# Group norm of the RWKV layer: sums, squares and normalisation moved from wide VectorE operations to ScalarE in blocks of 64 columns

## The chip, the cores and the metric

The kernel runs on one core of one Trainium2 chip. The metric is the device time of one execution in microseconds (us). PE is the matrix engine (TensorE), DVE VectorE, ACT ScalarE, POOL GpSimd, SP the engine that here only issues transfers.

## The reference

A decoder trunk of two residual layers, one sequence of 512 tokens, width 2048, all float32. Layer 0 is gated differential attention, layer 1 a gated RWKV-7 time mixing with 32 heads of 64. Layer 1, cut to what matters:

```python
p = h @ w_in;  p = p + (token_shift(p) - p) * mu       # r, k, v, g, and low-rank parts
y = wkv7_scan(r, decay, k, v, -kk, kk * a)             # (512, 32 heads, 64)
mean = jnp.mean(y, axis=-1, keepdims=True)
var = jnp.mean(jnp.square(y - mean), axis=-1, keepdims=True)
y = (y - mean) * lax.rsqrt(var + GN_EPS)
y = y * gn_w + gn_b + jnp.sum(r * k * r_k, axis=-1, keepdims=True) * v
out = (y * silu(g)) @ w_out
```

The change concerns the mean, the variance and the normalisation of `y`, per token and head.

## The kernel before

**Layer 1.** `layer1` runs over 16 pairs of heads (j = 0 to 15); the two heads of a pair have 128 channels. For each pair `unit_chan` makes four projections (k, r, v, gate) of 128 columns each, in matmuls of 128x512. Each product of float32 is three matmuls of split operands: `split_w` takes a loaded weight block `wraw`, writes its rounded part `wh` on ACT (L105) and the rest `wl` on DVE (L106), two buffers of each. `shift_mix` takes a projection out of PSUM and mixes it with its shifted self (L1187 on ACT, L1188 on DVE: mixr, mixk, mixv). `stage1` and `stage2` make the decays `E` and the tiles `AR` and `BK`; AR's second half (L1334) needs mixr.

**Gram and solve.** `gram` multiplies BK with AR in 16 matmuls (L1361), ACT copies the four results into `G` (L1368), and two blocks of G and the key norms `ssl` go through DRAM (`ltd`) into the tile `LT`, issued by POOL (L1407). `t_solve` inverts triangular blocks of 32 by a chain of small DVE operations that starts at L1409 and ends at L1429 (L1420 and L1422 by turns). The result goes through DRAM again (`td`, L1430, and `TT`, L1449, both issued by SP).

**The scan of the pair before.** A `Chain` is a generator whose steps are put in among the projections' matmuls, after a given number of them. `t_combine` transposes TT on DVE (L1459, tile `T1`, two instructions), multiplies with G (L1465, bank `px`), copies the result `X` on ACT (L1468), multiplies again (L1476) and copies it into TT (L1479). `scan_pair` then has eight steps of three matmuls each: L1558 (ACT copies `rhs`, L1561), L1569 with rhs and TT (ACT copies `VS`, L1571), and L1576 (DVE writes the next state VS, L1580 or L1583). After the eighth step `outputs` writes Y, two PSUM banks of 128 tokens x 4 blocks x 64 (L1598, L1602), and `centre` follows.

**The group norm.** `centre` sums Y over 64 columns (L1613, `s1`), scales the sum (L1614) and subtracts it (L1615), all on DVE, into `yc`, 128 tokens x 8 groups x 64. `group_norm` squares yc on ACT in one instruction (L1624), and on DVE sums the squares (L1626), makes `var` (L1627), its reciprocal root `rsg` in 11 small operations (`rsqrt`, L64 to L71), and multiplies (L1630). `finish_y` later transposes yc on PE (L1637) and adds it to the pair's `y`.

**Order.** Each engine's queue is in order. The order is set by a scheduler from the program's text, priorities (`high_priority`, `issue_after`) and its own estimates of durations, so that a change in one place can move instructions of others. `group_norm` of pair j - 2 is called at the head of pair j from j = 4 on.

Of the kernel before, what the change touches and what calls it, by code (L numbers as in the profile page):

```python
# [13 lines left out]
F32 = mybir.dt.float32  # L14
# [3 lines left out]
AF = mybir.ActivationFunctionType  # L18
ALU = mybir.AluOpType
AX = mybir.AxisListType  # L20
# [3 lines left out]
P = 128  # L24
# [3 lines left out]
NT = T // P  # L28
# [29 lines left out]
def rsqrt(g, out, v, n, tag):  # L58

    nc = g.nc  # L60
    m = 1 if tag in ("r4", "r16") else 3 if tag == "r8" else 2
    sh = g.small.tile([P, n], I32, name="rs_i", tag=tag + "i", bufs=m)
    t = g.small.tile([P, n], F32, name="rs_t", tag=tag + "t", bufs=m)
    nc.vector.tensor_single_scalar(sh[:], v.bitcast(I32), 1, ALU.logical_shift_right)  # L64
    nc.vector.tensor_scalar(sh[:], sh[:], -1.0, float(0x5F3759DF), ALU.mult, ALU.add)
    y = sh[:].bitcast(F32)
    for i in range(3):
        nc.vector.tensor_mul(t[:], y, y)
        nc.vector.scalar_tensor_tensor(t[:], t[:], -0.5, v, ALU.mult, ALU.mult)
        o = out if i == 2 else y  # L70
        nc.vector.scalar_tensor_tensor(o, t[:], 1.5, y, ALU.add, ALU.mult)  # L71
# [1120 lines left out]
C = 64  # L1192
NC_ = T // C
HALF = 32
NG = 4
# [351 lines left out]
def scan_pair(g, j, p, gap, gap_s, others):  # L1547
# [8 lines left out]
    for c in range(NC_):  # L1556
# [29 lines left out]
        yield gap_s  # L1586
    outputs(g, j, p)
    centre(g, p)


# [15 lines left out]
def centre(g, p):  # L1606

    nc, w, Y = g.nc, g.work, p.Y
    s1 = g.small.tile([P, NT, 2], F32, name="s1", tag="s1", bufs=3)
    p.yc = w.tile([P, 2 * NT, C], F32, name="yc", tag="yc", bufs=1)  # L1610
    for h in range(2):
        yg = Y[h][:, : NT * C].rearrange("p (t n) -> p t n", t=NT)
        nc.vector.reduce_sum(s1[:, :, h], yg, AX.X)  # L1613
        nc.vector.tensor_scalar(s1[:, :, h], s1[:, :, h], 1.0 / C, None, ALU.mult)  # L1614
        c = nc.vector.tensor_sub(p.yc[:, h::2, :], yg, s1[:, :, h : h + 1].to_broadcast([P, NT, C]))  # L1615
    g.centred = c.ins


def group_norm(g, j, p):
    p.chain.finish(g)  # L1620
    nc, w, yc = g.nc, g.work, p.yc
    NG = 2 * NT
    sq = w.tile([P, NG, C], F32, name="ysq", tag="ysq", bufs=1)
    nc.scalar.activation(sq[:], yc[:], AF.Square)  # L1624
    var = g.small.tile([P, NG], F32, name="var", tag="var", bufs=3)
    nc.vector.reduce_sum(var[:], sq[:], AX.X)  # L1626
    nc.vector.tensor_scalar(var[:], var[:], 1.0 / C, GN_EPS, ALU.mult, ALU.add)  # L1627
    rs = g.small.tile([P, NG], F32, name="rsg", tag="rsg", bufs=3)
    rsqrt(g, rs[:], var[:], NG, "r8")
    nc.vector.tensor_mul(yc[:], yc[:], rs[:, :, None].to_broadcast([P, NG, C]))  # L1630


def finish_y(g, j, p, bank=("pd", 1)):
# [8 lines left out]
def layer1(g, aps):  # L1642
    nc, tc = g.nc, g.tc
    with ExitStack() as cx:
# [32 lines left out]
        for j in range(D // P):  # L1677
# [16 lines left out]
            if normed:  # L1694
                group_norm(g, j - 2, pairs[j - 2])

            def behind(m, j=j, p=p, normed=normed):
                if j > 1:
                    pairs[j - 2].chain.finish(g)
                with tc.issue_after(m.ins):  # L1700
                    gram(g, j, p, j > LAG + 1 and pairs[j - 1].chain)
                with tc.issue_after(g.lower) if normed else ExitStack():
                    p.rfs = split_act(g, p.rf[:], w, "x")
                mask_gram(g, p, 0)
                loaded = t_solve(g, j, p, LAG < j < D // P - 1)
                with tc.issue_after(loaded):
                    mask_gram(g, p, 1)
                if j > 1 and not normed:
                    group_norm(g, j - 2, pairs[j - 2])
# [17 lines left out]
        chain(g, j, p, 24, 4, 5, lead=34)  # L1727
        gps = proj(3, j - 1)
        group_norm(g, j - 1, pairs[j - 1])
        gts = [gate(g, j - 1, gps)]  # L1730

# [140 lines left out]
```

## Time and profile before

| | |
|---|---|
| median of 3 runs (lowest, highest) | 2056.24 us (2054.85, 2058.01) |
| profiled execution, its time and span | 2055.6 us, 2053.9 us |
| granted TensorE clock | 1.0 |
| busy: PE, DVE, ACT, POOL | 99%, 78%, 55%, 19% of the span |
| second layer's pairs | about 1040 to 1930 us of the span |

The span is the time from the first to the last instruction; the profiled execution's own time has the launch around it. Times in the profile's rows count from the span's start. A row of a group of instructions gives the line in the kernel, the engine, the operation, output and inputs with their shapes, the count, then busy time, the mean of one in ns, and the idle time of the engine just ahead of them with what ended it. Rows in order of time give start, duration and, in brackets, the idle time before.

### The profile page before, as it was taken

The numbers are of one execution on the slowest core, as the hardware profiler recorded it, in microseconds if no ns is written. First come the engines' busy times: TensorE is split into PE (matmuls) and PEld (weight loads), VectorE is DVE, ScalarE is ACT, GpSimd is POOL, SyncE is SP. The second block draws the span as 40 slices with busy tenths as digits, with TensorE's granted clock in tenths as the row PEclk, the third lists the DMA queues.
The fourth block names the chain that finished last, engine by engine and source line by source line (L and its number), as shares of the span: only waits on it lengthen the run. The fifth ranks groups of instructions, "written<-read, shape, count | busy, mean of one in ns | idle before, by whom it ended". The sixth has DMA issues, their size and how long they took to land.

```text
span 2053.9 us, 34174 instructions
## 1 busy us (share of the span) xinstructions
PE 2035.2 (99%) x11922; PEld 1673.1 (81%) x11922; DVE 1605.9 (78%) x4100; ACT 1133.6 (55%) x2258; POOL 400.3 (19%) x782
## 2 busy tenths in 40 slices
PE   9999999999999999999999999999999999999999
PEld 7888888888888888888877778888888888877887
DVE  7988988888898977476787888787777888777745
ACT  5765656666666544355565555555555555545423
POOL 1020111102011000121222222322222222231011
PEclk9999999999999999999999999999999999999999
DMA  8487978879787965823333323223333232346676
GB/s 288 156 163 192 182 172 186 164 192 167 190 180 171 274 218 172 175 87 108 103 83 92 94 77 98 92 89 98 98 98 98 87 96 83 111 127 201 212 182 145
DMA packets 159534, 297.76 MB, mean 145 GB/s; under 512 B 64529, under 2 KB 81937, under 8 KB 159361
## 3 DMA queue, kind: packets, MB, share of 16 engines
q1 hardware_dynamic: 110768, 184.39, 28.8%
q0 software_dynamic: 25952, 90.88, 23.2%
q10 hardware_dynamic: 22640, 20.30, 3.1%
q8 instruction: 94, 1.54, 0.3%
q14 instruction: 80, 0.65, 0.1%
HBM read 271.33 MB, written 24.18 MB: 144 GB/s over the span
## 4 chain that ended last, share of the span: by engine, by line
PE 90%; DVE 6%; ACT 2%; issue 1%; DMA 1%; SPq 0%; ACTq 0%; DVEq 0%
PE pp L124 45%; PE pp L574 24%; PE pt L124 5%; PE gp L1361 2%; DVE wl L106 2%; PE sm L1558 1%; PE sc L124 1%; PE o L124 1%; PE sm L1576 1%; PE sm L1569 1%; ACT wh L105 1%; PE Y L1598 1%; PE pt L296 1%; PE z L124 1%; PE pt L1393 1%
## 5 line engine op out<-in xcount | busy, mean ns | idle before, releaser
L106 DVE TENSOR_TENSOR wl<-wraw,wh 128x1024 fp32r<-128x1024 f32 (+1 forms) x286 | 349.7, 1223 | 167.7 <-ACT wh L105 157.0
L105 ACT CAST wh<-wraw 128x1024 fp32r<-128x1024 f32 (+1 forms) x286 | 299.5, 1047 | 237.6 <-PE pp L124 115.8
L124 PE MATMUL pp<-hL,wh 128*128 128x512 f32 x1024 | 413.6, 404 | 0.0
L124 PE MATMUL pp<-hH,wl 128*128 128x512 f32 x1024 | 413.0, 403 | 0.0
L124 PE MATMUL pp<-hH,wh 128*128 128x512 f32 x1024 | 412.3, 403 | 0.2 <-ACT wh L105 0.2
L124 PEld LDWEIGHTS pp<-hH,wh 128*128 128x128 f32 x1024 | 193.1, 189 | 34.5 <-ACT wh L105 0.4
L124 PEld LDWEIGHTS pp<-hL,wh 128*128 128x128 f32 x1024 | 193.1, 189 | 33.5
L124 PEld LDWEIGHTS pp<-hH,wl 128*128 128x128 f32 x1024 | 193.2, 189 | 32.4
L574 PE MATMUL pp<-wh,hH 128*128 128x512 f32 x448 | 176.8, 395 | 0.0
L574 PE MATMUL pp<-wh,hL 128*128 128x512 f32 x448 | 175.8, 392 | 0.0
L124 PE MATMUL pp<-wh,hH 128*128 128x512 f32 x376 | 147.0, 392 | 0.6 <-ACT hH L1147 0.6
L124 PE MATMUL pp<-wl,hH 128*128 128x512 f32 x376 | 147.5, 392 | 0.0
L124 PE MATMUL pp<-wh,hL 128*128 128x512 f32 x376 | 147.3, 392 | 0.1
L1420 DVE SCALAR_TENSOR_TENSOR tmpl<-LT,Tm 128x60 f32<-128x60 f32 (+24 forms) x496 | 134.8, 272 | 13.2
L574 PE MATMUL pp<-wl,hH 128*128 128x512 f32 x448 | 140.3, 392 | 0.0
L1564 POOL COPY SA<-VS 64x64 f32<-64x64 f32 x224 | 55.4, 248 | 397.8 <-DVE VS L1580 375.4
L1422 DVE TENSOR_TENSOR Tm<-Tm,tmpl 128x60 f32<-128x60 f32 (+24 forms) x496 | 103.4, 209 | 11.7
L1561 ACT COPY rhs<-sm 64x64 f32<-64x64 f32 x256 | 53.0, 207 | 84.8 <-PE sm L1558 81.8
L574 PEld LDWEIGHTS pp<-wl,hH 128*128 128x128 f32 x448 | 84.5, 189 | 17.2
L574 PEld LDWEIGHTS pp<-wh,hH 128*128 128x128 f32 x448 | 84.2, 188 | 17.5 <-issue 0.4
L574 PEld LDWEIGHTS pp<-wh,hL 128*128 128x128 f32 x448 | 84.3, 188 | 16.1
L1571 ACT COPY VS<-sm 64x64 f32<-64x64 f32 x256 | 52.9, 207 | 76.2 <-PE sm L1569 70.3
(435 smaller groups left out, 4374.4 us busy)
## 6 DMA issues: line engine op xcount, KB each, us to landing
wraw<-in_rw_w_in_dram SPq DMA_DIRECT2D x128, 512.0 KB
wraw<-in_da_w_in_dram SPq DMA_DIRECT2D x75, 512.0 KB
wraw<-in_da_w_in_dram POOLq DMA_DIRECT2D x28, 512.0 KB, 6.6
wraw<-in_da_w_out_dram SPq DMA_DIRECT2D x26, 512.0 KB
wraw<-in_rw_w_out_dram SPq DMA_DIRECT2D x24, 512.0 KB
Ta<-in_da_w_in_dram POOLq DMA_DIRECT2D x21, 512.0 KB, 5.6
Tb<-in_da_w_in_dram POOLq DMA_DIRECT2D x21, 512.0 KB, 5.7
Tc<-in_da_w_in_dram POOLq DMA_DIRECT2D x21, 512.0 KB, 5.5
```

The source lines that it names most:

```text
L105: a = nc.scalar.copy(hi[:, ks], raw[:, ks])
L106: d = nc.vector.tensor_sub(lo[:, ks], raw[:, ks], hi[:, ks].bitcast(F32))
L124: m = nc.tensor.matmul(out, a, b, start=s, stop=e, skip_group_check=skip)
L296: nc.tensor.transpose(pt[:, c * P : (c + 1) * P], t1s[t][:, c * P : (c + 1) * P], g.ident[:])
L574: m = nc.tensor.matmul(out[t][:], x, wt[lo][:, k, :], start=first, stop=end and lo == 1 and k == KG - 1, skip_group_check=True)
L1361: m = nc.tensor.matmul(gp[h][:, i * P : (i + 1) * P], BK[r_, c0 + i, :, :], p.AR[r_, c0 + i, :, :], start=True, stop=True)
L1393: nc.tensor.transpose(ps[:, i * P : (i + 1) * P], p.BK[:, c0 + i].rearrange("p s t -> p (s t)"), g.ident[:])
L1420: nc.vector.scalar_tensor_tensor(tt, LT[:, i : i + 1, i + 1 :].to_broadcast([P, s, n]), n2[:, i : i + 1], Tm[:, 0:s, i : i + 1].to_broadca ...
L1422: nc.vector.tensor_add(Tm[:, 0:s, i + 1 :], Tm[:, 0:s, i + 1 :], tt)
L1561: nc.scalar.copy(rhs[r_, :], sm[r_, h * C : h * C + C])
L1564: nc.gpsimd.tensor_copy(p.SA[r_, c - 1, :], VS[r_, c, h, :])
L1571: g.copied = nc.scalar.copy(VS[r_, c, h, :], sm[r_, P : P + C])
```

## The change

The sums of Y are accumulated by eight ACT copies of 64 columns (L1612 in the changed kernel), out of PSUM into `yc`, which is no longer centred; one DVE operation turns the eight sums into minus the means (L1614, `p.mean`). Eight ACT squares (L1624) take minus the mean as bias and accumulate the variance. One small DVE product makes minus mean times `rsg` (L1628), and eight ACT instructions (L1630) normalise yc with it as bias and rsg as scale.

```diff
@@ -1606,14 +1606,12 @@
 def centre(g, p):
 
     nc, w, Y = g.nc, g.work, p.Y
-    s1 = g.small.tile([P, NT, 2], F32, name="s1", tag="s1", bufs=3)
+    p.mean = g.small.tile([P, 2 * NT], F32, name="s1", tag="s1", bufs=3)
     p.yc = w.tile([P, 2 * NT, C], F32, name="yc", tag="yc", bufs=1)
-    for h in range(2):
-        yg = Y[h][:, : NT * C].rearrange("p (t n) -> p t n", t=NT)
-        nc.vector.reduce_sum(s1[:, :, h], yg, AX.X)
-        nc.vector.tensor_scalar(s1[:, :, h], s1[:, :, h], 1.0 / C, None, ALU.mult)
-        c = nc.vector.tensor_sub(p.yc[:, h::2, :], yg, s1[:, :, h : h + 1].to_broadcast([P, NT, C]))
-    g.centred = c.ins
+    for i in range(2 * NT):
+        nc.scalar.activation(p.yc[:, i], Y[i % 2][:, i // 2 * C : i // 2 * C + C], AF.Copy,
+                             accum_out=p.mean[:, i : i + 1])
+    g.centred = nc.vector.tensor_scalar(p.mean[:], p.mean[:], -1.0 / C, None, ALU.mult).ins
 
 
 def group_norm(g, j, p):
@@ -1621,13 +1619,15 @@
     nc, w, yc = g.nc, g.work, p.yc
     NG = 2 * NT
     sq = w.tile([P, NG, C], F32, name="ysq", tag="ysq", bufs=1)
-    nc.scalar.activation(sq[:], yc[:], AF.Square)
     var = g.small.tile([P, NG], F32, name="var", tag="var", bufs=3)
-    nc.vector.reduce_sum(var[:], sq[:], AX.X)
+    for i in range(NG):
+        nc.scalar.activation(sq[:, i], yc[:, i], AF.Square, bias=p.mean[:, i : i + 1], accum_out=var[:, i : i + 1])
     nc.vector.tensor_scalar(var[:], var[:], 1.0 / C, GN_EPS, ALU.mult, ALU.add)
     rs = g.small.tile([P, NG], F32, name="rsg", tag="rsg", bufs=3)
     rsqrt(g, rs[:], var[:], NG, "r8")
-    nc.vector.tensor_mul(yc[:], yc[:], rs[:, :, None].to_broadcast([P, NG, C]))
+    nc.vector.tensor_mul(p.mean[:], p.mean[:], rs[:])
+    for i in range(NG):
+        nc.scalar.activation(yc[:, i], yc[:, i], AF.Identity, bias=p.mean[:, i : i + 1], scale=rs[:, i : i + 1])
 
 
 def finish_y(g, j, p, bank=("pd", 1)):
```

ACT, the end of one pair's scan and the head of the next, a period of the middle of layer 1, before. L1468 to L1479 belong to t_combine, L1561 and L1571 to the first step of the scan, L1368 to gram:

```order
L1571 COPY VS<-sm 64x64 x2
L1624 ACTIVATE ysq<-yc 128x512
L105 CAST wh<-wraw 128x1024
L1187 ACTIVATE mixr<-pp,omu 128x512
L1468 COPY X<-px 32x256 x2
L1348 COPY ssl<-pt 128x128
L1156 CAST sHx<-mixr 128x512
L1368 COPY G_14182<-gp 128x8x64 x4
L1479 COPY TT_9496<-px 32x8x32 x2
L105 CAST wh<-wraw 128x1024
L1561 COPY rhs<-sm 64x64 x2
L1571 COPY VS<-sm 64x64 x2
```

and after, where the eight copies and four of the squares come ahead of mixr and the weight cast, and six of the eight normalisations ahead of TT, all eight ahead of rhs:

```order
L1571 COPY VS<-sm 64x64 x2
L1612 ACTIVATE yc,s_14157<-Y 128x64 x8
L1624 ACTIVATE ysq,var<-yc,s_14157 128x64 x4
L1187 ACTIVATE mixr<-pp,omu 128x512
L105 CAST wh<-wraw 128x1024
L1624 ACTIVATE ysq,var<-yc,s_14157 128x64 x4
L1468 COPY X<-px 32x256 x2
L1348 COPY ssl<-pt 128x128
L1156 CAST sHx<-mixr 128x512
L1368 COPY G_14284<-gp 128x8x64 x2
L1630 ACTIVATE yc<-yc,s_14157,rsg 128x64 x6
L1479 COPY TT_9496<-px 32x8x32 x2
```

ACT goes on, after, with the other two normalisations, the next weight cast and the scan's first step:

```order
L1630 ACTIVATE yc<-yc,s_14157,rsg 128x64 x2
L105 CAST wh<-wraw 128x1024
L1561 COPY rhs<-sm 64x64 x2
L1368 COPY G_14284<-gp 128x8x64 x2
L1571 COPY VS<-sm 64x64 x2
```

Two of gram's four copies of G have moved behind rhs. DVE, between the v projection's mix (mixv) and the start of the solve (L1409), before:

```order
L1188 SCALAR_TENSOR_TENSOR mixv<-pp,mu,mixv 128x511
L1491 TENSOR_TENSOR y<-pt,mixv 128x512
L1580 SCALAR_TENSOR_TENSOR VS<-sm,gam,Sg 64x64 x2
L1409 TENSOR_SCALAR LT<-LT 128x32
L1410 RECIPROCAL LT<-LT 128x32
L1420 SCALAR_TENSOR_TENSOR tmpl<-LT,Tm 128x31
```

and after, where a weight split and the state of scan step 2 come ahead of the solve:

```order
L1188 SCALAR_TENSOR_TENSOR mixv<-pp,mu,mixv 128x511
L1491 TENSOR_TENSOR y<-pt,mixv 128x512
L1580 SCALAR_TENSOR_TENSOR VS<-sm,gam,Sg 64x64 x2
L106 TENSOR_TENSOR wl<-wraw,wh 128x1024
L1580 SCALAR_TENSOR_TENSOR VS<-sm,gam,Sg 64x64 x2
L1409 TENSOR_SCALAR LT<-LT 128x32
L1410 RECIPROCAL LT<-LT 128x32
L1420 SCALAR_TENSOR_TENSOR tmpl<-LT,Tm 128x31
```

DVE at the head of a period, after. L1524 and L1531 belong to the gate of an earlier pair, L1459 are the two transposes:

```order
L1429 TENSOR_TENSOR Tm<-Tm,LT 128x256
L1524 SCALAR_TENSOR_TENSOR mixv<-thg,mixv 128x512
L1531 TENSOR_TENSOR mixv<-mixv,y 128x512
L1614 TENSOR_SCALAR s_14157<-s_14157 128x8
L1188 SCALAR_TENSOR_TENSOR mixr<-pp,mu,mixr 128x511
L1459 STREAM_TRANSPOSE T_14189<-TT_9496 64x256
L106 TENSOR_TENSOR wl<-wraw,wh 128x1024
L1459 STREAM_TRANSPOSE T_14189<-TT_9496 64x256
L1334 TENSOR_TENSOR AR<-mixr,E 128x8x64
L1625 TENSOR_SCALAR var<-var 128x8
L1335 SCALAR_TENSOR_TENSOR mixr<-mixr,prm_hrk,f 128x512
```

Before, the two transposes stood together directly behind centre's L1615; now the scaled sums (L1614) stand behind the solve's last instruction, and a weight split stands between the transposes.

## The prediction

> **What bounds the kernel now.** I read the busy shares first, then the busy time by stretch, then the chain that ended last inside one period of the second layer, and then ACT's and DVE's instructions of that period in order of time.
>
> ```profile
> PE 2035.2 (99%) x11922; PEld 1673.1 (81%) x11922; DVE 1605.9 (78%) x4100; ACT 1133.6 (55%) x2258; POOL 400.3 (19%) x782
> ```
>
> ```profile
> 1040.00:1278.00 238.00, 233.02 (x1732) 189.23 (x1732) 190.87 (x534) 132.69 (x311) 64.06 (x158) 1.00 0.32 92
> 1278.00:1808.00 530.00, 530.00 (x3834) 438.89 (x3833) 418.75 (x1160) 294.14 (x674) 142.89 (x342) 1.00 0.33 97
> 1808.00:1930.00 122.00, 119.16 (x807) 93.26 (x806) 86.47 (x216) 60.01 (x136) 27.43 (x59) 1.00 0.54 172
> ```
>
> The second fence is busy time by stretch (length, then PE, PEld, DVE, ACT, POOL, the granted clock, DMA). The change lies in these three stretches. In the middle one, nine equal periods, TensorE is busy for all 530.00 us: nothing done there by another engine can shorten it. TensorE's idle time in the other two is 238.00 - 233.02 = 5.0 and 122.00 - 119.16 = 2.8 us. So the change can gain at most about 8 us, and what it can lose is TensorE time in which the in-order PE queue stands in front of a matmul of the scan whose operand is late. One period of that queue, from the chain that ended last:
>
> ```profile
> 1342.37 0.62 PE px L1465 x32
> ...
> 1343.35 1.99 PE gp L1361 x32
> ...
> 1345.96 2.06 PE pp L124 x8
> ...
> 1349.64 0.17 PE sm L1569 x2
> ```
>
> PE does L1465 (needs DVE's transposes T1), the Gram products, L1476 (needs ACT's X), eight projection matmuls, and at 1349.64 L1569, the first step of the next scan, which needs ACT's TT and rhs. ACT at the same time (start, us, instruction, idle before it):
>
> ```profile
> 1331.80 0.44 ACT L1571 COPY VS<-sm 64x64 f32<-64x64 f32 x2
> 1336.74 0.63 ACT L1624 ACTIVATE ysq<-yc 128x512 f32<-128x512 f32 x1 [4.50 <-DVE yc L1615]
> 1338.10 1.05 ACT L105 CAST wh<-wraw 128x1024 fp32r<-128x1024 f32 x1 [0.73 <-PE pp L124]
> 1339.18 0.69 ACT L1187 ACTIVATE mixr<-pp,omu 128x512 f32<-128x512 f32 x1
> 1343.07 0.74 ACT L1468 COPY X<-px 32x256 f32<-32x256 f32 x2 [3.19 <-PE px L1465]
> ...
> 1344.00 0.62 ACT L1156 CAST sHx<-mixr 128x512 fp32r<-128x512 f32 x1
> 1344.52 2.06 ACT L1368 COPY G<-gp 128x512 f32<-128x512 f32 x4
> 1346.43 0.73 ACT L1479 COPY TT<-px 32x256 f32<-32x256 f32 x2
> 1347.42 1.05 ACT L105 CAST wh<-wraw 128x1024 fp32r<-128x1024 f32 x1 [0.26 <-ACT TT L1479]
> 1348.49 0.43 ACT L1561 COPY rhs<-sm 64x64 f32<-64x64 f32 x2
> 1349.84 0.43 ACT L1571 COPY VS<-sm 64x64 f32<-64x64 f32 x2 [0.93 <-PE sm L1569]
> ```
>
> The reader is to see two things. Up to 1343.07 ACT has 4.50 + 0.73 + 3.19 = 8.4 us of idle time. From 1343.07 to rhs, ending at 1348.92, it has almost none, and PE takes rhs at 1349.64: 0.7 us of slack.
>
> **The prices.**
>
> ```profile
> L1561 ACT COPY rhs<-sm 64x64 f32<-64x64 f32 x256 | 53.0, 207 | 84.8 <-PE sm L1558 81.8
> L281 ACT ACTIVATE t<-t,rr 128x128 f32<-128x128 f32 x64 | 21.2, 393 | 9.0 <-DVE rr L277 9.0
> L1319 ACT ACTIVATE k<-mixk,prm_kk 128x512 f32<-128x512 f32 x16 | 11.5, 721 | 0.3
> L1304 ACT ACTIVATE f<-th,prm_omka,prm_hka 128x512 f32<-128x512 f32 x16 | 12.8, 800 | 0.0
> ```
>
> ```profile
> 344.07 1.28 ACT L281 ACTIVATE t<-t,rr 128x128 f32<-128x128 f32 x4 [0.30 <-DVE rr L277]
> ...
> 377.29 0.46 ACT L350 ACTIVATE a<-sc,nb,sq 128x128 f32<-128x128 f32 x1 [0.87 <-DVE nb L347]
> 377.64 0.19 ACT L350 ACTIVATION_READ_ACCUMULATOR a<-sc,nb,sq 128x1 f32 x1
> 377.74 1.04 ACT L105 CAST wh<-Td 128x1024 fp32r<-128x1024 f32 x1
> ```
>
> No instruction of 64 columns with pointer operands is in this trace, so the prices are estimates from these rows. L1561 is a copy of 64 columns out of PSUM: 0.207 us, which I take for the first eight, since they read PSUM too. With one [128,1] operand L281 (128 columns) and L1319 (512) differ by (721 - 393) / 384 = 0.854 ns a column, so 64 columns take 393 - 55 = 338 ns; that is a square. A second operand adds 800 - 721 = 79: 417 ns, a normalisation. Four L281 in a row take 1.28 us, so each starts (1.28 - 0.393) / 3 = 0.296 after the one before, an overlap of 0.097; a normalisation then occupies 0.32. Where a sum is accumulated, the read follows and the next instruction starts at 377.74, 0.45 after a 0.46 instruction: the read costs the overlap and no more, so copy and square occupy 0.21 and 0.34. Per pair: 8 x 0.21 + 8 x 0.34 + 8 x 0.32 = 7.0 us, in place of one square of 0.63. Over 16 pairs ACT gets about 102 us more.
>
> The Trainium skill, ScalarE: Activation LUTs, section What ACT_TABLE_LOAD costs, gives 186 ns + 0.833 ns a column, 93 ns more for each pointer operand, and 93 ns of overlap back to back. By it the estimate is 8 x (239 + 333 + 333) ns = 7.2 us, with the copies dearer than the 207 ns that the trace has for L1561; the 0.3 us of difference falls on the copies, which lie in idle time, so the sum would stay.
>
> ```profile
> L1613 DVE TENSOR_REDUCE s<-Y x32: 411/416/425, 1047.9 to 1909.0; 128x4 f32<-128x256 f32 x32
> L1615 DVE TENSOR_TENSOR yc<-Y,s x32: 411/416/425, 1049.3 to 1909.9; 128x256 f32<-128x256 f32 x32
> L1630 DVE TENSOR_TENSOR yc<-yc,rsg x16: 681/692/1610, 1055.0 to 1915.3; 128x512 f32<-128x512 f32 x16
> ```
>
> DVE loses 2 x 0.416 + 2 x 0.416 + 0.69, and about as much as the last for the sum of the squares over as many columns: 3.0 us a pair, 49 us in all. It is worth nothing by itself: in the middle stretch DVE is busy 418.75 of 530 us and PE all of it.
>
> **Place 1, from the scan's end to X: hidden.** ACT is free at 1332.24, the outputs Y are complete at 1335.09 (below). Copies to 1336.8, the scaling of the sums on DVE (behind the solve's tail, below), four squares, mixr, the weight cast wh, four squares: 1.7 + 0.3 + 1.4 + 0.6 + 1.05 + 1.4 ends at about 1342, before X can start. The work fits into the 8.4 us of idle time; wh is later, but PE's queue has 32 projection matmuls there, up to 1342.37, that run on the other buffer.
>
> **Place 2, from X to rhs: on the path.** With T the time at which PE can start L1465, DVE's order after it is AR, var, mixr, the rsqrt's small operations with sLx between, and the product of mean and rsg:
>
> ```profile
> 1335.09 0.76 DVE L1613 TENSOR_REDUCE s<-Y 128x4 f32<-128x256 f32 x2 [1.95 <-PE Y L1602]
> ...
> 1338.28 0.17 DVE L1627 TENSOR_SCALAR var<-var 128x8 f32<-128x8 f32 x1
> 1338.48 0.17 DVE L64 TENSOR_SCALAR rs_i<-var 128x8 int32<-128x8 int32 x1
> ...
> 1341.32 0.69 DVE L1334 TENSOR_TENSOR AR<-mixr,E 128x512 f32<-128x512 f32 x1
> ...
> 1342.05 0.75 DVE L1335 SCALAR_TENSOR_TENSOR mixr<-mixr,prm_hrk,f 128x512 f32<-128x512 f32 x1
> ```
>
> Small operations start 0.20 apart, so 13 of them take 2.6, and the three wide ones (two of 0.69, one of 0.75, each overlapping the next by some 0.08) 1.9: mean is ready at T + 4.5. ACT does X, ssl, sHx and two G copies up to T + 0.7 + 1.45 + 1.03 = T + 3.2, and then stands, because its next six instructions are normalisations. They run to T + 4.5 + 1.9 = T + 6.4; TT to T + 7.1; two more to T + 7.8; wh to T + 8.8; rhs to T + 9.2. PE reaches L1569 at T + 1349.64 - 1342.37 = T + 7.3. So PE stands for 1.9 us in each such period, and everything behind it in its queue with it. Bounds: with normalisations as short as L1561 the eight take 0.9 less, 1.0 us; without overlap (0.42 each) and with mean 0.5 late, 3.2 us. I take 1.9, the rows being near. The last two G copies now stand behind rhs, but VS of the next step waits for L1569 anyway, and they feed the Gram exchange, next.
>
> **Place 3, the solve.** In the new DVE order a weight split wl and the scan's VS of step 2 come ahead of the solve's first instruction, L1409:
>
> ```profile
> 1300.29 0.18 DVE L1409 TENSOR_SCALAR LT<-LT 128x32 f32<-128x32 f32 x1
> ...
> 1303.96 1.23 DVE L106 TENSOR_TENSOR wl<-wraw,wh 128x1024 fp32r<-128x1024 f32 x1
> ...
> 1330.04 0.42 DVE L1429 TENSOR_TENSOR Tm<-Tm,LT 128x256 f32<-128x256 f32 x1
> ```
>
> That wl cannot start before 1303.96, since its cast waits for PE to free a buffer; with wl and VS (two of 0.29) the solve starts at 1305.7 instead of 1300.29, 5.4 late. Its body is dense on DVE, one VS step (0.6) fewer and a small split (0.4) more stands in it, and one wl leaves and one enters: it ends 5.2 late. What is late next is the block TT, which goes through two transfers:
>
> ```profile
> 1388.98 0.42 DVE L1429 TENSOR_TENSOR Tm<-Tm,LT 128x256 f32<-128x256 f32 x1
> 1396.18 0.44 DVE L1459 STREAM_TRANSPOSE T<-TT 64x256 f32<-64x256 f32 x1 [0.20 <-DMA TT<-td]
> ```
>
> The period is 1388.98 - 1330.04 = 58.94. The second transpose ends at 1396.6, and PE wants it at 1342.37 + 58.94 = 1401.3: a slack of 4.7. After the change it comes 5.2 late and 1.15 more, because wl now stands between the two transposes: T is 5.2 + 1.15 - 4.7 = 1.7 us late, and PE stands that long before L1465. Bounds: nothing, if the transfers (7.2 us from L1429 to this transpose) run 2 us faster with fewer weight loads ahead of them; 3, if they run as much slower as the trace's other periods differ. I take 1.7. The Gram exchange that feeds the solve is late by its last G copy, at T + 10.2, and must be through before the solve's new, later start; the solve's own 5.4 us and PE's standing cover it.
>
> **Sum.** Eleven pairs (3 to 13) have the new ACT order, ten of them follow a delayed solve: 11 x 1.9 + 10 x 1.7 = 38 us. For the first three and the last two pairs, whose order mixes the same instructions in otherwise, I take two such stalls, 4 us (0 to 8). Together 42 us on the profiled execution's 2055.6, which is 0.6 below the median: 2056.2 + 42 = 2098 us.
>
> **Rivals.**
> - Place 3 costs nothing, because the transfers shrink: 11 x 1.9 + 4 = 25, 2081 us. For it: SP has no load between the two transfers now. Against it: the slack of 4.7 is smaller than the shift of the solve alone. 15%.
> - All of it is hidden: within 4 us, 2056. It needs the normalisations not to stand ahead of TT and rhs; the order says they do, and the slack there is 0.7 us. 6%.
> - Faster. DVE's 3.0 us a pair come off a chain that PE waits on: outside the middle stretch PE's idle 5.0 + 2.8 us vanish, 2048 us. This decides where mean and TT come earlier, not later, that is if the copies took less than DVE's part by over 1 us. 5%. The Trainium skill, Perfetto Trace Analysis, section Optimization Strategies, says to unload the engines that block an idle TensorE; no row of the middle stretch shows such idle time.
> - ACT becomes the bound: all 102 - 10 us that it gets appear in the span, 2148. For it: ACT is in order and feeds PE's weights. Against it: 294 busy of 530 us in the middle stretch, and the 8.4 us of idle time in place 1. 7%.
>
> **How the numbers follow.** My forecast has the other 67%. Its own range, by the bounds above, is 11 x 1.0 + 0 = 11 to 11 x 3.2 + 10 x 3 + 8 = 73 us; ends that all fall together are unlikely, and I take 2068 to 2122, which also takes in the first rival and leaves out 18%. A measurement of this kernel tells apart about 0.2%, 4 us; slower by more than that has 67 + 15 + 7 = 89%, the same 6%, faster 5%.
>
> **What would show it.** Right: a new idle time of PE ahead of L1569, released by ACT's rhs, near 2 us in eleven periods, and one ahead of L1465, released by DVE's transposes; L1409 about 5 us later in its period; ACT without idle time between the scan's end and X; a middle stretch in which PE is no longer busy throughout. Wrong: a span under 2062, PE waiting for the weight casts instead, or normalisations that take far from 0.4 us each.

## The result and the profile after

The changed kernel takes 2129.57 us (median of 4 runs, 2125.92 to 2132.16) against 2055.61 us before (2054.85 to 2058.01): a ratio of 1.0359, 95% interval 1.0346 to 1.0371. It is 74 us slower, where 42 were forecast. The profiled execution took 2132.16 us with a span of 2130.5, 76.6 us longer than the span of before, and that difference is what is taken apart here.

The page's busy line, and the same three stretches of time that the prediction showed of before:

```profile
PE 2069.8 (97%) x11922; PEld 1694.0 (80%) x11922; DVE 1567.3 (74%) x4004; ACT 1236.1 (58%) x2882; POOL 407.2 (19%) x782
```

```profile
1040.00:1278.00 238.00, 229.21 (x1641) 184.67 (x1640) 172.11 (x482) 154.87 (x459) 62.44 (x150) 0.99 0.30 88
1278.00:1808.00 530.00, 500.42 (x3509) 409.32 (x3508) 361.35 (x1010) 318.60 (x941) 133.39 (x309) 0.97 0.29 87
1808.00:1930.00 122.00, 113.15 (x797) 90.04 (x796) 77.55 (x221) 69.95 (x223) 34.65 (x76) 0.96 0.37 110
```

ACT has 102.5 us more and DVE 38.6 less. In the middle stretch PE was busy for all 530.00 us; now it is busy for 500.42, and the column behind POOL, the granted clock, has gone from 1.00 to 0.97. The view by core says the same of the whole span:

```profile
core 0: 2130.5 us, clock 0.987
```

So there are two losses, and a view for each. A stand is here an idle time of PE ahead of one instruction. The waits of PE (who waits, for which line, us in total, times, longest):

```profile
PE sm L1569 <- ACT rhs L1561: 32.0, 13, 3.3
PE px L1465 <- DVE T L1459: 8.5, 7, 2.1
PE sm L1558 <- DVE VS L1580: 7.1, 17, 0.9
```

In the kernel before these three lines had 2.0, 2.0 and 2.8 us. PE's idle time in the span, span less busy, was 2053.9 - 2035.2 = 18.7 us and is 2130.5 - 2069.8 = 60.7: 42.0 us more. The clock is seen in PE's instructions in order of time (start, us, instruction, idle before it), here around one stand ahead of L1569:

```profile
1365.37 0.39 PE L124 MATMUL pp<-hH,wh 128*128 128x512 f32 x1
1365.60 0.39 PE L124 MATMUL pp<-hL,wh 128*128 128x512 f32 x1
1369.13 0.46 PE L1569 MATMUL sm<-rhs,TT 128*128 128x64 f32 x2 [3.15 <-ACT rhs L1561]
...
1369.93 0.63 PE L124 MATMUL pp<-hH,wh 128*128 128x512 f32 x1
1370.35 0.63 PE L124 MATMUL pp<-hL,wh 128*128 128x512 f32 x1
```

Ahead of the stand, matmuls of 512 columns start 0.23 us apart; behind it 0.42. I read the granted clock in stretches of 1 us over the whole span: it is 1.00 or 0.50, and at 0.50 always for 3.41 us or a multiple of that. Sixteen such windows are in this trace, ten single ones between 1178 and 1827, each behind a stand at L1569, one at 1752 behind a wait of 1.33 us at L1465, and five after 1888. A window that PE works through at half rate costs 1.71 us: 27.3 us in all, or 26.6 without the 1.5 us in which PE was idle inside them. The kernel before has none but the last 0.9 us of its span, where PE has no work left. The number is not the same in every execution: of the four runs, the two with a mean clock of 0.987 took 2132 us and the two with 0.990 took 2126 and 2127, and 0.003 of the span, 6 us, would be some four windows (an estimate from these clocks).

42.0 + 27.3 = 69.3 of the 76.6 us. The other 7.3 must be PE time that the profile books as busy. Part of it can be seen: a matmul in front of a stand shows its whole modelled 0.39 us (1365.60) where in a dense queue the next one starts 0.23 after it, so such a stand is about 0.16 us longer than its idle time says. The list has 37 of them at these three lines, 28 more than before: 4.5 us. What is left, some 3 us, is not taken apart.

### The profile page after: what moved, and what is told of

Read it like the earlier page. It is cut to its first block, busy times and chain, and to the rows that moved or that the text cites. A ratio compares the mean times of both kernels' runs of the same rounds, so it can differ in the third digit from the quotient of the medians.

```text
span 2130.5 us, 34746 instructions
## 1 busy us (share of the span) xinstructions
PE 2069.8 (97%) x11922; PEld 1694.0 (80%) x11922; DVE 1567.3 (74%) x4004; ACT 1236.1 (58%) x2882; POOL 407.2 (19%) x782
## 4 chain that ended last, share of the span: by engine, by line
PE 23%; DVE 18%; ACT 5%; DMA 3%; issue 3%; POOL 0%; DVEq 0%; SPq 0%; ACTq 0%; POOLq 0%
PE pp L124 15%; PE pt L124 4%; DVE tmpl L1420 4%; DVE wl L106 3%; DVE Tm L1422 3%; DMA td<-Tm 2%; ACT yc L1630 2%; DVE VS L1580 2%; ACT wh L105 1%; DMA TT<-td 1%; PE sm L1569 1%; PE sm L1558 1%; PE sm L1576 1%; DVE l L1295 1%; PE pt L1393 1%
## 5 line engine op out<-in xcount | busy, mean ns | idle before, releaser
L124 PE MATMUL pp<-hL,wh 128*128 128x512 f32 x1024 | 418.2, 408 | 0.0
L124 PE MATMUL pp<-hH,wh 128*128 128x512 f32 x1024 | 417.5, 408 | 0.1
L124 PE MATMUL pp<-hH,wl 128*128 128x512 f32 x1024 | 417.6, 408 | 0.0
L1420 DVE SCALAR_TENSOR_TENSOR tmpl<-LT,Tm 128x60 f32<-128x60 f32 (+24 forms) x496 | 135.0, 272 | 13.4
L1561 ACT COPY rhs<-sm 64x64 f32<-64x64 f32 x256 | 52.8, 206 | 93.6 <-PE sm L1558 91.2
L1571 ACT COPY VS<-sm 64x64 f32<-64x64 f32 x256 | 52.8, 206 | 69.5 <-PE sm L1569 63.1
```

What stands on the lines that cost most here:

```text
L124: m = nc.tensor.matmul(out, a, b, start=s, stop=e, skip_group_check=skip)
L1420: nc.vector.scalar_tensor_tensor(tt, LT[:, i : i + 1, i + 1 :].to_broadcast([P, s, n]), n2[:, i : i + 1], Tm[:, 0:s, i : i + 1].to_broadca ...
L1561: nc.scalar.copy(rhs[r_, :], sm[r_, h * C : h * C + C])
L1571: g.copied = nc.scalar.copy(VS[r_, c, h, :], sm[r_, P : P + C])
```

## The experiments

Theory A, formed from the two traces: what costs are the queue places, that is the normalisations ahead of TT and rhs on ACT and the later solve on DVE, and the half clock that follows a long stand; the added work itself is free. Theory B: ACT's added 102 us show in proportion, since ACT feeds PE's weights. The first four kernels tell these apart. Theory G, from the fifth on, is A with a rule for the clock: time is divided into windows of 3.41 us on a fixed grid, and a window in which PE was busy for less than half is followed by one at half clock.

**All the work on ACT, the normalisations late.** The changed kernel, but the eight normalisations are issued behind the VS copy of scan step 1, out of the way of rhs, and `finish_y`, which reads them, moves from step 0 to step 3 (not shown).

```diff
+    def normalise():
+        for i in range(NG):
+            nc.scalar.activation(yc[:, i], yc[:, i], AF.Identity, bias=p.mean[:, i : i + 1], scale=rs[:, i : i + 1])
...
+    with tc.issue_after(g.last_copy.ins):
+        q.normalise()
```

> The changed kernel, with the eight normalisations of a pair queued on ACT behind scan step 1 instead of ahead of TT and rhs, and finish_y moved from step 0 to step 3. All of ACT's added work (about 100 us) is still there. Theory A (the time is lost where the normalisations stand ahead of rhs, in the solve that starts later, and in the halved TensorE clock after PE has stood for 3 us): all three vanish, 2055 to 2066 us. Theory B (ACT's added busy time shows in the span in proportion, wherever it stands): still about 2130 us.

Measured: 2069.21 us, ratio 1.0061 (1.0044 to 1.0078). With every instruction of the change on ACT, 61 of 74 us are gone, so B is wrong. The time is above A's range by 3 us. From one L1476 to the next the middle periods last 59.6 to 59.7 us where before they lasted 58.9, some 6 us over the middle stretch, of which 3.3 are idle time. About 5 us more lie in the last pairs, where PE's longest wait is now

```profile
PE pt L1643 <- ACT yc L1632: 3.9, 2, 3.5
```

the late normalisation of a pair whose output PE transposes at 1880, with one window at half clock behind it.

**The sums alone, the squares alone, the normalisation alone.** Each is the kernel before with one third of the change.

```diff
 # sums only (centre)
-    nc.vector.reduce_sum(s1[:, :, h], yg, AX.X)
+    nc.scalar.activation(p.yc[:, i], Y[i % 2][:, i // 2 * C : i // 2 * C + C], AF.Copy, accum_out=s1[:, i : i + 1])
 # squares only (group_norm)
-    nc.scalar.activation(sq[:], yc[:], AF.Square)
-    nc.vector.reduce_sum(var[:], sq[:], AX.X)
+    nc.scalar.activation(sq[:, i], yc[:, i], AF.Square, accum_out=var[:, i : i + 1])
 # normalisation only (group_norm)
-    nc.vector.tensor_mul(yc[:], yc[:], rs[:, :, None].to_broadcast([P, NG, C]))
+    nc.scalar.activation(yc[:, i], yc[:, i], AF.Copy, scale=rs[:, i : i + 1])
```

> The kernel before, with only the sums of Y accumulated by eight ACT copies of 64 columns; subtraction, squares and normalisation stay wide as before. A: the copies lie in ACT's idle time before X: within 4 us of before. B: 8 x 0.20 us x 16 pairs = 26 us of ACT work, of which 74/103 as in the changed kernel, +18 us.

> The kernel before, with only the squares taken by eight ACT instructions that accumulate the variance. A: they lie in ACT's idle time before X: within 4 us of before. B: (8 x 0.24 - 0.53) us x 16 = 22 us of ACT work, +16 us.

> The kernel before, with only the last multiplication made by eight ACT instructions with rsg as scale. In ACT's order they stand behind ssl, ahead of all four G copies, TT and rhs. A: 8 x 0.24 = 1.9 us, less the 0.7 us of slack, that is 1.2 to 1.8 us in each of some 12 pairs, without a fall of the granted clock (PE stands for less than 3 us at a time): 2070 to 2080 us. B: 31 us of ACT work, +22 us, 2078, but with no new wait of PE ahead of L1569.

Measured: 2059.0 (1.0014, 1.0005 to 1.0023), 2059.19 (1.0017, 1.0007 to 1.0026) and 2086.8 us (1.0147, 1.0129 to 1.0165). Sums and squares cost 3 us each, most of it at the last pair (L1637 waits 2.7 and 2.6 us in all, 1.0 before, with a window at half clock behind), so place 1 was indeed all but hidden. The normalisation alone costs 31, more than A had allowed:

```profile
PE sm L1569 <- ACT rhs L1561: 20.1, 13, 2.6
```

Its copies of TT and rhs stand behind eight normalisations, its solve is where it was, and PE stands 1.0 to 2.6 us ahead of L1569. This is place 2 alone, though in an order of its own: all four copies of G also stand ahead of rhs. Five windows at half clock (8.5 us) come on top of 21.2 us more idle time. Not every stand halved the clock: one of 1.98 us did, one of 2.44 did not. That asked for the next kernels.

**Stands without the work.** The kernel before, only with the two idempotent copies of TT (L1479) issued 6, 8 or 10 times in the middle pairs (8 is shown).

```diff
-    for h, b0, lo, _ in blocks:
+    for h, b0, lo, _ in blocks * (8 if LAG < j < D // P - 1 else 1):
         nc.scalar.copy(TT[lo, :, h, HALF:C], px[lo, N:].rearrange("p (c s) -> p c s", c=NC_))
```

> The kernel before, its means, squares and normalisation untouched; only ScalarE's two copies of TT (L1479) are issued six times in the pairs of the middle, so that rhs comes later and TensorE stands about 1.6 us ahead of L1569 in some 12 pairs. Theory G (the granted clock is set for windows of 3.41 us on a fixed grid; a window in which TensorE stood 1.7 us or more is followed by one at half clock, which costs 1.71 us; nothing else of the change matters): 12 stands of 1.6 us, no fall of the clock or one or two: 2056 + 19 + 3 = 2078 us (2070 to 2085), mean clock 0.998 to 1.000. Rival R (every stand of over 1 us halves the clock): 12 falls of 1.71 us on top, 2098 us, clock 0.99. Rival S (the clock has to do with what ScalarE and VectorE run, not with the stand): no fall, 2078 us.

> The same with the two copies issued eight times and TensorE standing about 3.0 us in some 12 pairs, as long as in the changed kernel; no work of the second layer is moved to ScalarE. Theory G: 12 x 3.0 = 36 us of standing, and about 10 windows at half clock, 17 us: 2056 + 36 + 17 + 4 = 2113 us (2100 to 2122), mean clock 0.99. Rival S (no fall without the moved work): 2096 us, clock 1.000.

> The kernel before with the two TT copies issued ten times in the pairs of the middle: TensorE stands some 3.3 us ahead of L1569 in 12 pairs, where eight times gave 2.08 us. Theory G (a window of 3.41 us of a fixed grid in which TensorE was busy for less than half is followed by one at half clock): a stand of 3.3 us leaves such a window at nearly every phase of the grid, 10 to 12 falls, 12 x 3.3 + 11 x 1.71 + 3 = 62 us, 2117 us (2105 to 2130), clock about 0.99. Rival S (the three falls in the middle at 2.08 us were chance, and the falls of the changed kernel came with its moved work): 3 falls, 2104 us.

Measured: 2086.12 (1.0149, 1.0133 to 1.0164), 2092.2 (1.0184, 1.0167 to 1.0201) and 2106.07 us (1.025, 1.0232 to 1.0267). The waits of each, in this order:

```profile
PE sm L1569 <- ACT TT L1479: 18.0, 12, 1.7
```

```profile
PE sm L1569 <- ACT TT L1479: 25.2, 12, 2.4
```

```profile
PE sm L1569 <- ACT TT L1479: 30.1, 12, 2.8
```

The stands came out as 1.5, 2.1 and 2.5 us on average, not 1.6, 3.0 and 3.3. The first time is 1 us above its range, the second 8 below it and the third at the low end of its own. The second and third stands were shorter than meant. The first time is high because a stand costs more than its idle time: without a window at half clock the periods last 61.1, 61.5 and 62.0 us, where before they lasted 58.9, so stands of 1.45, 2.08 and 2.49 us cost 2.2, 2.6 and 3.1. What the runs decide is who halves the clock. Without any moved work there are 2, 4 and 8 windows at half clock (one in each kernel behind a wait at the last pairs), more with longer stands; rival S (the moved work) falls, and so does R (every stand of over 1 us), with 2 where 12 would have been. Theory G's size, 10 falls, was not reached either. Its rule is seen in the windows of the grid themselves. From the run with eight copies, three windows around each of two stands, both 2.08 us long (length, PE, PEld, DVE, ACT, POOL, clock):

```profile
1602.49:1605.90 3.41, 2.90 (x14) 2.05 (x12) 0.00 (x0) 3.18 (x11) 1.34 (x4) 1.00 0.13 23
1605.90:1609.32 3.42, 1.85 (x14) 1.57 (x15) 0.80 (x1) 3.26 (x8) 0.93 (x2) 1.00 0.49 150
1609.32:1612.73 3.41, 3.41 (x18) 2.84 (x17) 1.65 (x4) 1.56 (x4) 2.47 (x5) 1.00 0.46 151
```

```profile
1663.93:1667.34 3.41, 2.96 (x14) 2.12 (x13) 0.00 (x0) 3.20 (x10) 1.76 (x4) 1.00 0.20 35
1667.34:1670.76 3.42, 1.79 (x14) 1.50 (x14) 0.74 (x1) 3.24 (x9) 0.57 (x2) 1.00 0.47 143
1670.76:1674.17 3.41, 3.41 (x12) 2.73 (x11) 1.72 (x4) 0.29 (x1) 2.40 (x5) 0.50 0.42 151
```

The same stand fell on the grid 0.07 us differently; 1.85 us of PE time in the window kept the clock, 1.79 lost it. In the changed kernel a stand of 3.15 us filled one window almost whole:

```profile
1366.00:1369.42 3.42, 0.28 (x3) 0.29 (x3) 0.75 (x1) 3.32 (x9) 0.00 (x0) 1.00 0.00 0
1369.42:1372.83 3.41, 3.41 (x12) 2.85 (x12) 0.57 (x2) 1.06 (x4) 1.77 (x2) 0.50 0.46 113
```

I laid such a grid through the eleven kernels that have a window at half clock (one phase for each), 3354 windows in the second layer, and sorted those at full clock by PE's busy time. Under 1.70 us: 35, of which 33 were followed by half clock. From 1.70 to 2.12: 33, of which 6, five of them with a stand of only 1.3 to 1.5 us. Above: 3242, none. What decides between 1.70 and 2.12 stays open.

**The normalisations on ACT behind all four copies of G; and on DVE.** Both keep sums and squares on ACT.

```diff
 # gram first: normalise() as above, and behind the pair's last copy of G (L1368)
+    with tc.issue_after(g.gram_copy):
+        pairs[j - 2].normalise()
 # normalisation on DVE
-    nc.vector.tensor_mul(p.mean[:], p.mean[:], rs[:])
-    for i in range(NG):
-        nc.scalar.activation(yc[:, i], yc[:, i], AF.Identity, bias=p.mean[:, i : i + 1], scale=rs[:, i : i + 1])
+    nc.vector.tensor_add(yc[:], yc[:], p.mean[:, :, None].to_broadcast([P, NG, C]))
+    nc.vector.tensor_mul(yc[:], yc[:], rs[:, :, None].to_broadcast([P, NG, C]))
```

> The changed kernel with all its sums, squares and normalisations on ScalarE, but the eight normalisations are issued behind the pair's fourth copy of G (L1368): solve in its old place, four copies of G and then TT ahead of the first two normalisations. Theory G: rhs waits for two normalisations and two copies of G in place of eight normalisations and comes about 0.4 us after TensorE wants it, no window at half clock: 2056 + 12 x 0.5 + 7 = 2069 us (2060 to 2080), clock 0.998 or more, against 2130 for the changed kernel. Rival B (ScalarE's added 102 us show wherever they stand): 2130 us. Rival C (each normalisation or copy of G ahead of rhs shows in full): 1.7 us in 12 pairs, 2083 us.

> The changed kernel with sums and squares on ScalarE, and the normalisation by two wide operations on VectorE. Theory G: nothing stands ahead of rhs that did not before; the small losses of the sums alone and of the squares alone (3.4 and 3.6 us) add up: 2062 us (2056 to 2070), clock 0.999. Rival B (ScalarE's added busy time, here 50 us of the 102): 2090 us.

Measured: 2071.92 (1.008, 1.0065 to 1.0095) and 2059.55 us (1.0022, 1.0012 to 1.0031). Their middle stretches:

```profile
1278.00:1808.00 530.00, 529.84 (x3820) 435.42 (x3819) 393.19 (x1102) 350.58 (x1020) 140.51 (x342) 1.00 0.33 95
```

```profile
1278.00:1808.00 530.00, 530.00 (x3833) 438.98 (x3832) 407.86 (x1114) 326.32 (x952) 144.91 (x342) 1.00 0.33 97
```

In the first, ACT does all of the change, 350.58 us in this stretch, and PE is idle for 0.16 us of it. Its periods there last 59.2 to 59.3 us, 0.3 longer than before, so in the middle pairs all but 0.3 us a pair was a loss of order, and the rivals B (2130) and C (2083) fall. Some 14 of its 17 us lie at the two ends (stands of 1.8 and 2.0 us at 1177 and 1239, 4.0 at 1884, three windows at half clock), so my split of them, 0.5 us in each of 12 pairs and 7 beside, was wrong though the time was in range. The second kernel costs 4 us, in its range, 3.35 of standing at the last pair's transposes and the window behind it.

**The later solve alone.** The kernel before, with the solve's first part behind the VS of scan step 2 on DVE.

```diff
-    with g.tc.high_priority(offset=SOLVE), g.tc.issue_after(g.state.ins) if a and split else ExitStack():
+    with g.tc.high_priority(offset=SOLVE), g.tc.issue_after(g.state.ins) if split else ExitStack():
...
+    others[2] = (2, lambda p=p: (turn_values(g, p), next(p.solve)))
```

> The kernel before, with the solve's first part (L1409 to the 21st step) put behind the VS of scan step 2 on VectorE, where the changed kernel has it; means, squares and normalisation as before on VectorE. Place 3 alone. By the prediction's price (T 1.7 us late in 10 pairs): 17 us, 2073 us, all of it as standing of TensorE ahead of L1465. By what the changed kernel's trace shows (8.5 us ahead of L1465 in all, in 7 pairs): 6 to 9 us, 2064 us. The rival that the transfers shrink and place 3 costs nothing: within 3 us of 2056. No window at half clock in any of these, since the stands are under 1.7 us.

Measured: 2076.85 us, ratio 1.0107 (1.0092 to 1.0122): 22 us. The prediction's price was near, my later reading of the changed trace too low, and there is one window at half clock after all, at 1176 behind a stand of 2.0 us. Not all of PE's new standing is ahead of L1465 (two lines are added above, so L1467 is L1465, L1560 is L1558 and L1478 is L1476):

```profile
PE sm L1560 <- DVE VS L1582: 8.2, 16, 0.9
PE px L1467 <- DVE T L1461: 5.5, 11, 2.0
```

Before, these two lines had 2.8 and 2.0 us. From one L1478 to the next, the middle periods last 60.2 to 60.7 us where before they lasted 58.9. In the one from 1355.35, PE loses some 0.6 us of the 1.7 ahead of L1467 and 0.7 around one L1560. DVE and PE there, in order of time:

```profile
1387.74 0.23 DVE L1420 TENSOR_TENSOR Tm<-Tm,tmpl 128x64 f32<-128x64 f32 x1
1387.89 0.27 DVE L1582 SCALAR_TENSOR_TENSOR VS<-sm,gam,Sg 64x64 f32<-64x64 f32 x1
1388.08 0.28 DVE L1418 SCALAR_TENSOR_TENSOR tmpl<-LT,Tm 128x75 f32<-128x75 f32 x1
1388.39 0.29 DVE L1582 SCALAR_TENSOR_TENSOR VS<-sm,gam,Sg 64x64 f32<-64x64 f32 x1
...
1412.49 0.44 DVE L1461 STREAM_TRANSPOSE T<-TT 64x256 f32<-64x256 f32 x1
```

```profile
1388.83 0.46 PE L1560 MATMUL sm<-VS,G 128*128 128x128 f32 x2 [0.50 <-DVE VS L1582]
...
1412.98 0.69 PE L1467 MATMUL px<-T,G 32*32 32x32 f32 x30 [0.41 <-DVE T L1461]
```

The two halves of VS (L1582) stand in DVE's queue among the solve's steps (L1418, L1420), which run later in the period now, and PE waits for the second half. These stands seem not to lengthen the period, but to take up time that PE would else stand ahead of L1467. T, here the end of the second transpose, comes 57.6 us behind the pair's L1478 (1412.93 less 1355.35); before it came 51.3 behind L1476 (1396.62 less 1345.27). That is 6.2 us later, 1.5 more than the slack of 4.7. And from the weight split at 1372.92 to the solve's last instruction at 1404.09 no idle time of DVE is over 0.04 us, so PE's stands in between did not hold the solve up. This is read from the order of time; no run takes VS out of the solve's way.

## Why the prediction was wrong, and where it was right

The direction and the places were right. The sum agrees with the profile's idle time, 42 us forecast and 42.0 us more measured, but that is in part luck: L1569 has 30.0 us more where 21 were forecast, L1465 6.5 where 17 were, and L1558, for which the sum has no term, 4.3. The time lies outside the range because the sum has no term for the clock. That is the step that failed: "PE stands for 1.9 us in each such period, and everything behind it in its queue with it" prices a stand at its own length. In the changed kernel every stand of 1.77 us or more also brought at least one window of 3.41 us at half clock. The sixteen windows cost some 27 us, without which the time would have been about 2102, inside the range, and the runs with repeated TT copies show the fall of the clock with nothing else changed. The Trainium skill, TensorE: Matmul & The Clock Gate, section What's actually happening, gives the window, free-running, 3413 ns, and half clock after at least one idle window. The length and the grid agree with these traces (windows of 3.41 us, a whole number of them apart). By its rule of an idle window, though, stands of 1.9 to 3.2 us would have cost nothing more; here a window that PE spent half idle was enough (33 of the 35 with under 1.70 us of PE time), and the measurement decides.

Taken by the prediction's steps:

- **Prices.** A normalisation was put at 417 ns, a square at 338 and a copy at 207. The rows (min/median/max) have

```profile
L1612 ACT ACTIVATE yc<-Y x128: 215/238/270, 1048.4 to 1986.6; 128x64 f32<-128x64 f32 x128
L1624 ACT ACTIVATE ysq<-yc,s x128: 332/336/413, 1050.5 to 1990.5; 128x64 f32<-128x64 f32 x128
L1630 ACT ACTIVATE yc<-yc,s,rsg x128: 423/427/443, 1057.4 to 1996.9; 128x64 f32<-128x64 f32 x128
```

  By the Trainium skill, ScalarE: Activation LUTs, section What ACT_TABLE_LOAD costs, the copy takes an estimated 239 ns; the row's 238 agrees. ACT's 102.5 us more are the 102 of the text. DVE lost 38.6, not 49, and either was worth nothing, as argued.
- **Place 1, hidden.** Right: 3 us each with the sums or the squares alone. The sign given for it was too strong: ACT is not without idle time there, but stands 3.01 us ahead of X in the period below (1359.42).
- **Place 2, 11 x 1.9 us.** The mechanism was right, the size too small: L1569's wait grew by 30.0 us where 21 were forecast; most stands are 2.8 to 3.3 us, near the upper bound of 3.2. One period of ACT and DVE after the change:

```profile
1359.42 0.74 ACT L1468 COPY X<-px 32x256 f32<-32x256 f32 x2 [3.01 <-PE px L1465]
...
1360.86 1.07 ACT L1368 COPY G<-gp 128x512 f32<-128x512 f32 x2
1364.18 2.10 ACT L1630 ACTIVATE yc<-yc,s,rsg 128x64 f32<-128x64 f32 x6 [2.24 <-DVE s L1628]
1366.18 0.72 ACT L1479 COPY TT<-px 32x256 f32<-32x256 f32 x2
1366.93 0.77 ACT L1630 ACTIVATE yc<-yc,s,rsg 128x64 f32<-128x64 f32 x2
1367.61 1.03 ACT L105 CAST wh<-wraw 128x1024 fp32r<-128x1024 f32 x1
1368.66 0.42 ACT L1561 COPY rhs<-sm 64x64 f32<-64x64 f32 x2
```

```profile
1360.07 0.58 DVE L64 TENSOR_SCALAR rs_i<-var 128x8 int32<-128x8 int32 x1
1360.68 0.64 DVE L65 TENSOR_SCALAR rs_i<-rs_i 128x8 int32<-128x8 int32 x1
...
1363.64 0.17 DVE L1628 TENSOR_TENSOR s<-s,rsg 128x8 f32<-128x8 f32 x1
```

```profile
1359.47 1.15 POOL L1472 COPY G<-AR 64x512 f32<-64x512 f32 x1 [3.67 <-PE px L1465]
1360.67 0.61 POOL L1472 COPY G<-AR 64x512 f32<-64x512 f32 x1
```

  The order is the forecast one. L1476 starts at 1361.65 here, 2.97 us behind T as before, so T is 1358.68. The mean is ready at 1363.81, T + 5.1 and not 4.5, and ACT starts 0.37 later: of the 1.2 us by which rhs (T + 10.4, forecast 9.2) is later than worked out, these are 1.0. A small part is a reading: the 1349.64 at which the prediction has PE take rhs comes from the view of the chain, and in PE's own order of time L1569 starts at 1349.47 (L1465 at 1342.30), so the slack was 0.55 us and not 0.7. The two integer steps of the rsqrt take 0.58 and 0.64 where before they took 0.17 each (1338.48); in the new order they meet POOL's two copies of G, and each ends 0.03 to 0.04 us after one of the copies does (1360.65 after 1360.62, 1361.32 after 1361.28). The Trainium skill, SBUF — State Buffer, section SBUF: two separate sides, has POOL and some operations of DVE (those in a two-port mode, or with two inputs in SBUF) share a pair of ports under an exclusive lock, the later one blocked until the other's instruction ends. These rows agree with it, but which mode L64 and L65 run in is in no row, and no run took the copies away.
- **Place 3, 10 x 1.7 us.** Near in the kernel with the later solve alone: the solve starts 19.5 us behind the pair's L1476 where before it starts 14.0, 5.5 later (forecast 5.4), T is 1.5 beyond its slack (forecast 1.7), and the kernel loses 22 us. What the text did not have is that PE stands part of it ahead of the scan's VS, which is queued behind the solve on DVE. In the changed kernel L1465 waits seven times, not ten. L1465 and L1558 wait 6.5 and 4.3 us more than before, together 10.8, where the later solve alone has 3.5 and 5.4, together 8.9; what place 3 costs inside the changed kernel is not separated.
- **The rivals.** ACT as the bound, at 2148, is nearest to the measured time and wrong as a mechanism: with all its work and another order the middle stretch was full. DVE's relief was worth nothing: none of the runs was faster than before.

Places 2 and 3 alone cost 31 and 22 us, together 53; the change costs 74. Some 17 of the 21 us that are more are the clock: 8.5 and 1.7 us of it apart, 27.3 together. By the count of windows above, stands of 1.0 to 2.6 us mostly leave a window half busy and stands of 2.8 to 3.3 mostly don't.

## What to carry to other kernels

Where TensorE is busy all the time, moving work to an engine with idle time is free only if it goes in behind what TensorE waits for: the same 102 us on ScalarE cost 0.3 us a pair in the middle behind the last copy of G, and some 6 us a pair ahead of TT and rhs, with the solve later too. Price a stand of TensorE at somewhat more than its idle time (0.5 to 0.7 us more in the kernels with repeated copies). Add the chance of a window at half clock, here 1.7 us each: it was seen from stands of 1.3 us on, seldom below 1.7, and at every stand of 2.8 us or more; it can nearly double a stand of 2 us. Of an operation that moves on one engine, follow also who is queued behind it there: with the later solve, the larger part of TensorE's new waits stood ahead of a scan step behind it (5.4 of 8.9 us).

## What was not expected of the hardware

- The granted clock knew only 1.00 and 0.50 in these traces, changed at steps of 3.41 us that run through a whole execution, and fell after 33 of 35 windows with under 1.70 us of PE time. It came back after one busy window, but 5 of 44 windows at half clock were followed by another; four of those five still held some idle time of PE, 2.79 to 3.00 of 3.41 us busy; in the fifth PE was busy throughout.
- Two small integer operations of DVE took 0.58 and 0.64 us instead of 0.17, up to the end of a POOL copy each, as told above.
